# Five of each expert's 84 weight halves as native fp32 matmuls, in a kernel that splits every weight into two fp32r parts

## The chip, the cores and the metric

The kernel runs on one core of one Trainium2 chip. The metric is the device time of one execution in microseconds. Of the kernel before three runs are given, 1871.48, 1871.95 and 1874.96 us, with a median of 1871.95 us.

## The reference, cut to what matters

Two decoder blocks are applied to 256 tokens of 1024 features, in fp32: a hybrid layer (convolution, two kinds of attention, a state-space branch, and a feed-forward), then a retention layer with a dense feed-forward and a Fourier layer with a mixture of experts. The change lies in that last part alone:

```
def moe_swiglu(h, w_router, w_gate, w_up, w_down):
    t = h.reshape(-1, d)
    logits = (t @ w_router).astype(jnp.float32)
    top_val, top_idx = lax.top_k(logits, TOP_K)          # 2 of 8 experts
    top_w = jax.nn.softmax(top_val, axis=-1)
    ...
    for e in range(N_EXPERTS):
        out = out + gates[:, e:e + 1] * swiglu(t, w_gate[e], w_up[e], w_down[e])
```

An expert has a gate and an up matrix of 1024 x 3584 and a down matrix of 3584 x 1024, so 44 MB of fp32 weights; `swiglu(t)` is `(silu(t @ w_gate) * (t @ w_up)) @ w_down`.

## The kernel before

**Weights.** They arrive as units of 128 x 2048 fp32 (1 MB) in a ring of raw tiles, in the order of use: 42 units, 84 halves of 128 x 1024, for an expert. `split` (line 117) turns a half into two fp32r tiles: ScalarE copies it to `wh` (line 128), VectorE subtracts, `wl = raw - wh` (line 129). The tiles come from the pool `wp` with four buffers of each (`WB = 4`, line 77), so the wh of a half can be written once TensorE has read the wh of the split half four before it. After the second half of a unit, `fetch` (line 94) has SP issue the next unit into the raw tile that comes free. `half` (line 171) splits one half more and hands out the oldest of the queue `wq`.

**Order.** The instructions of TensorE and SP stand as the program writes them; a scheduler sets those of VectorE and ScalarE.

**An expert.** `gather` (line 1075) builds one-hot matrices `so` from the routing (four VectorE operations, line 1082) and with them picks the expert's tokens, up to 128, as `ex` (hi and lo part, 8 blocks of features). Its pieces are called by hooks at halves 77 to 83 of the expert before. `experts` (line 1116) then runs seven rounds s = 0 to 6:
- `gate_strip(s)`: halves g0 to g3, each with two of the eight feature blocks. `hi_lo` (line 1133) makes three matmuls of 128 x 512 for a block: ex-hi with wh (line 1142), ex-lo with wh (1143), ex-hi with wl (1144). Between g1 and g2 of round s stands `turn(s - 1)`, the transposes of the round before (lines 1194 and 1196). ScalarE evacuates the sum as `sg` (line 1177).
- `up_strip(s)`: halves u0 to u3; VectorE evacuates it as `h` = up x sg (line 1184).
- `down(s - 1)`: halves d0 to d3, with the turned tokens `hx` (lines 1200 and 1201) of the round before.

So the halves run g, u, then six times g, u, d, and d of round 6 last. Up and down halves exist in two forms on TensorE, chosen at run time by the expert's count of tokens (`either`, line 1146): over 64 tokens, three matmuls a block as in the gate; else the hi and lo part of the tokens lie beside each other in one stationary operand, and two matmuls do (lines 1139 and 1144). Gate halves always have three. Below, the second kind of expert is called packed, and the halves of round s are written g0 to g3, u0 to u3, d0 to d3 (the d halves that run in a round belong to round s - 1). `combine` (line 1246) adds an expert's result to `acc`, as hooks at halves 4 and 8 of the next expert: two matmuls (lines 1251 and 1252) and a VectorE operation (line 1254) for each of two token tiles. Experts are counted from 0.

Native fp32 matmuls, of unsplit tiles, already stand in other places, such as line 786 in the retention layer (128 x 512, both operands fp32).

Of the kernel before, what the change touches and what calls it, by code (L numbers as in the profile page):

```python
# [9 lines left out]
F32 = mybir.dt.float32  # L10
F32R = mybir.dt.float32r
I32 = mybir.dt.int32
AF = mybir.ActivationFunctionType
# [3 lines left out]
P = 128  # L17
# [5 lines left out]
E = 8  # L23
# [3 lines left out]
UE = 42  # L27
# [36 lines left out]
def kernel(  # L64
# [10 lines left out]
    nc = tc.nc  # L75
    NU = ws_d.shape[0]
# [2 lines left out]
    HQ = 512  # L79
    HU = UN // 2  # L80

    NRAW, R2N, R3N, R4N = 6, 4, 2, 2
    const = ctx.enter_context(tc.tile_pool(name="const", bufs=1))
    rawp = ctx.enter_context(tc.tile_pool(name="rawp", bufs=NRAW))
# [5 lines left out]
    raw = []  # L90
    wq = []
# [23 lines left out]
    half_ = [0, 0]  # L115

    def split(scales=None, between=None):


        if not raw or (half_[1] == H_F2 and scales is None):  # L120
            return
        half_[1] += 1
        r = raw[0][0][:, half_[0] * HU:(half_[0] + 1) * HU]
        wh = wp.tile([P, HU], F32R, tag="wh", name="wh")
        wl = wp.tile([P, HU], F32R, tag="wl", name="wl")
        if scales is None:
            for o in (slice(0, HQ), slice(HQ, HU)) if half_[1] == 1 else (slice(0, HU),):
                nc.scalar.activation(out=wh[:, o], in_=r[:, o], func=AF.Copy)  # L128
                nc.vector.tensor_tensor(out=wl[:, o], in0=r[:, o], in1=wh[:, o].bitcast(F32), op=ALU.subtract)  # L129
                if between is not None and o.start == 0:  # L130
                    between()
        else:
            for t in range(2):
                o = slice(t * 512, t * 512 + 512)
                nc.scalar.activation(out=wh[:, o], in_=r[:, o], func=AF.Copy, scale=scales[:, t:t + 1])
                nc.vector.scalar_tensor_tensor(out=wl[:, o], in0=r[:, o], scalar=scales[:, t:t + 1],
                                               in1=wh[:, o].bitcast(F32), op0=ALU.mult, op1=ALU.subtract)
        wq.append((wh, wl))
        if half_[0]:
            fetch(raw.pop(0)[1])  # L140
        half_[0] ^= 1
# [39 lines left out]
    def bank(tag="mm", shape=(P, 2, S)):  # L181
        return psp.tile(list(shape), F32, tag=tag, name=tag, bufs={"mm": 4, "sd": 2, "dn": 2}[tag])

    mm = nc.tensor.matmul
# [175 lines left out]
    start = ExitStack()  # L360
# [12 lines left out]
    with pa:  # L373
# [264 lines left out]
        for i in range(8):  # L638
            ps = unitT(xh, xl)
            c, h = divmod(i, 2)  # L640
# [28 lines left out]
        for c in range(4, KD, 2):  # L669
            gg = []  # L670
            for _ in range(2):
                g = B.tile([P, 4, S], F32, tag="gate2", name="gate2")
                for h in range(2):
                    ps = unitT(xh, xl)
# [63 lines left out]
    with ExitStack() as pr:  # L738
# [120 lines left out]
        for c in range(KD):  # L859
            ps = bank("mm", (P, S))  # L860
# [23 lines left out]
    with ExitStack() as pn:  # L884
# [90 lines left out]
        for cc in range(4):  # L975
            ps = unit_late(zh, zl) if cc == 0 else unitT(zh, zl)
# [34 lines left out]
        for c in range(0, KD, 2):  # L1011
            ps, o = to_tok(xT_, c, "mm")
            nc.scalar.activation(out=acc[:, :, o], in_=ps, func=AF.Copy)

        ps = bank("sd", (P, 3, E))
# [51 lines left out]
    with ExitStack() as pe:  # L1067
# [7 lines left out]
        def gather(posc, posuc):  # L1075

            so = G2.tile([P, 2, P], F32R, tag="so", name="so")
            for t in range(2):  # L1080
                for c, o in ((posc, slice(0, HS)), (posuc, slice(HS, P))):
                    nc.vector.tensor_scalar(out=so[:, t, o], in0=iota1[:, o], scalar1=c(t), scalar2=None, op0=ALU.is_equal)
            ex = G.tile([P, KD, 2, P], F32R, tag="ex", name="ex")
            sot = G2.tile([P, 2, P], F32R, tag="sot", name="sot")
            rs = G2.tile([P, 1], F32, tag="rsl", name="rsl")

            xs = {}

            def rows(hf):
                o = slice(hf * 512, hf * 512 + 512)  # L1090
                ps = bank("sd", (P, 512))
                for i, (src, t) in enumerate(((th, 0), (th, 1), (tl, 0), (tl, 1))):
                    mm(ps, so[:, t], src[:, t, o], start=i == 0, stop=i == 3)
                xs[hf] = G2.tile([P, 512], F32, tag=("sg", "h")[hf], name="xs", bufs=1)
                nc.scalar.activation(out=xs[hf], in_=ps, func=AF.Copy)

            def tokens_of(hf):
                ps = bank("sd", (P, 4, P))
                for b in range(4):
                    nc.tensor.transpose(ps[:, b], xs[hf][:, b * P:(b + 1) * P], ident)  # L1100
                ks = slice(4 * hf, 4 * hf + 4)
                nc.scalar.activation(out=ex[:, ks, 0], in_=ps, func=AF.Copy)
                nc.vector.tensor_tensor(out=ex[:, ks, 1], in0=ps, in1=ex[:, ks, 0].bitcast(F32), op=ALU.subtract)  # L1103

            def rest():
                ps = bank("sd", (P, 2 * P + 2))
                for t in range(2):
                    mm(ps[:, t * P:(t + 1) * P], so[:, t], identr, start=True, stop=True)
                for t in range(2):
                    mm(ps[:, 2 * P:2 * P + 1], so[:, t].bitcast(F32), rcol[:, t:t + 1], start=t == 0, stop=t == 1)  # L1110
                nc.vector.tensor_copy(out=rs, in_=ps[:, 2 * P:2 * P + 1])
                nc.vector.tensor_copy(out=sot.rearrange("p a b -> p (a b)"), in_=ps[:, 0:2 * P])

            return ex, sot, rs, [lambda: rows(0), lambda: tokens_of(0), lambda: rows(1), lambda: tokens_of(1), rest]

        def experts(ex, rs, half_fn, hooks=None, n_of=None):

            pd = [bank("dn", (P, 512)) for _ in range(2)]
            n = [0]
            few = [None]
# [2 lines left out]
            def nexth(**kw):  # L1127
                if hooks and n[0] in hooks:
                    hooks[n[0]]()
                n[0] += 1  # L1130
                return half_fn(**kw)

            def hi_lo(x, items, packed):

                for out_, k, wh, wl, first, last in items:
                    xk = x[:, k].rearrange("p a b -> p (a b)")
                    if packed:
                        e = xk[:, HS:HS + P]
                        mm(out_, e, wh, start=first, stop=False)  # L1139
                    else:  # L1140
                        e = xk[:, 0:P]
                        mm(out_, e, wh, start=first, stop=False)  # L1142
                        mm(out_, xk[:, P:2 * P], wh, start=False, stop=False)  # L1143
                    mm(out_, e, wl, start=False, stop=last)  # L1144
# [10 lines left out]
            def strip_items(ps, h, w):  # L1155
                return [(ps, 2 * h + kk, w[0][:, kk * 512:(kk + 1) * 512], w[1][:, kk * 512:(kk + 1) * 512],
                         h + kk == 0, h == 3 and kk == 1) for kk in range(2)]

            def strip(mid=None):
                ps = bank("mm", (P, 512))  # L1160
                for h in range(4):
                    if h == 2 and mid is not None:
                        mid()
                    hi_lo(ex, strip_items(ps, h, nexth()), False)
                return ps

            def pair(f):
# [100 lines left out]
        for e in range(E):  # L1268
            ex, sot, rs, _ = nxt
# [246 lines left out]
```

## Time and profile before

| what | value |
|---|---|
| median of three runs | 1871.95 us |
| the profiled execution | 1872.74 us, span 1871.0 us |
| granted TensorE clock, mean | 0.995 of full speed |
| TensorE busy | 1817.4 us, 97% of the span |
| VectorE busy | 1482.0 us, 79% |
| ScalarE busy | 1210.6 us, 65% |
| expert stage | from about 900 us to the end |
| moved from memory | 502.45 MB |

In the rows, PE is TensorE, DVE is VectorE, ACT is ScalarE and SP issues the DMAs; PEld is TensorE's loading of stationary operands. Matmuls are pipelined: a matmul row shows about 0.39 us, and the next one starts some 0.23 us after it, so durations of TensorE are taken from start to start. A native fp32 matmul shows as two records.

### The profile page before, as it was taken

The page shows a single profiled execution, that of the slowest core. Times are in us where ns is not written, and L with a number is a line of the kernel's source. Part 1 is how long each engine was busy: PE and PEld are TensorE (multiplying, and loading weights), DVE is VectorE, ACT ScalarE, POOL GpSimd, SP SyncE. Part 2 cuts the span into 40 slices and gives each one's busy share as a digit, 9 for nine tenths or more (in the row PEclk, how much of TensorE's full clock was granted, in tenths as well). Part 3 has the DMA queues.
Part 4 walks back from the last instruction along what each step waited for, and adds up shares of the span by engine and source line. Part 5 has one row for each costly group of instructions (what it writes and reads, how often), then busy time and mean ns, then how long its engine had stood idle before and what let it go on. Part 6 is the DMA issues. An engine that isn't in the chain of part 4 may idle for free. (4 is left out here: it accounts for less than half of the span.)

```text
span 1871.0 us, 28740 instructions
## 1 busy us (share of the span) xinstructions
PE 1817.4 (97%) x10890; PEld 1574.5 (84%) x10890; DVE 1482.0 (79%) x1855; ACT 1210.6 (65%) x1484; POOL 158.2 (8%) x154
## 2 busy tenths in 40 slices
PE   8999999999999999999999999999999999999997
PEld 7999999999888999998777887777777788888885
DVE  5666676657677666656899989999999998988987
ACT  5765454455344444446787777888878777777775
POOL 2302122211111122110000000000000000000000
PEclk9999999999999999999999999999999999999999
DMA  8344544555444564544799998999999999999970
GB/s 313 140 154 168 193 178 183 181 181 197 158 150 159 189 248 184 187 170 180 295 419 377 353 367 326 411 386 377 415 354 413 381 353 364 332 356 354 343 290 36
DMA packets 71156, 505.77 MB, mean 270 GB/s; under 512 B 7888, under 2 KB 8016, under 8 KB 10320
## 3 DMA queue, kind: packets, MB, share of 16 engines
q1 hardware_dynamic: 70992, 503.53, 70.7%
q8 instruction: 110, 1.80, 0.4%
q14 instruction: 54, 0.44, 0.1%
HBM read 502.45 MB, written 1.05 MB: 269 GB/s over the span
## 5 line engine op out<-in xcount | busy, mean ns | idle before, releaser
L129 DVE TENSOR_TENSOR wl<-raw,wh 128x1024 fp32r<-128x1024 f32 (+1 forms) x906 | 1078.5, 1227 | 235.3 <-ACT wh L128 226.2
L128 ACT ACTIVATE wh<-raw 128x1024 fp32r<-128x1024 f32 (+1 forms) x906 | 922.0, 1053 | 428.9 <-PE mm L190 188.7
L189 PE MATMUL mm<-xh,wh 128*128 128x256 f32 x1248 | 357.5, 286 | 6.7 <-ACT xh L342 6.7
L1144 PE MATMUL mm<-wl,ex 128*128 128x512 f32 x896 | 356.0, 397 | 3.7 <-DVE wl L129 3.7
L190 PE MATMUL mm<-xl,wh 128*128 128x256 f32 x1248 | 355.2, 285 | 1.0 <-DVE xl L343 0.7
L191 PE MATMUL mm<-xh,wl 128*128 128x256 f32 x1248 | 354.9, 284 | 0.8 <-DVE wl L129 0.8
L1142 PE MATMUL mm<-wh,ex 128*128 128x512 f32 x672 | 270.4, 402 | 0.0
L1143 PE MATMUL mm<-wh,ex 128*128 128x512 f32 x672 | 266.1, 396 | 0.2 <-DVE ex L1103 0.2
L189 PEld LDWEIGHTS mm<-xh,wh 128*128 128x128 f32 x1248 | 237.9, 191 | 8.2 <-ACT xh L342 6.7
L190 PEld LDWEIGHTS mm<-xl,wh 128*128 128x128 f32 x1248 | 237.9, 191 | 2.4 <-DVE xl L343 2.3
L191 PEld LDWEIGHTS mm<-xh,wl 128*128 128x128 f32 x1248 | 237.7, 190 | 1.1 <-DVE wl L129 1.0
L1144 PEld LDWEIGHTS mm<-wl,ex 128*128 128x128 f32 x896 | 168.6, 188 | 54.2 <-DVE wl L129 13.7
L1144 PE MATMUL dn<-wl,hx 128*128 128x512 f32 x448 | 183.6, 410 | 12.1 <-DVE wl L129 11.9
L1143 PEld LDWEIGHTS mm<-wh,ex 128*128 128x128 f32 x672 | 126.7, 189 | 28.2 <-DVE ex L1103 0.5
L1142 PEld LDWEIGHTS mm<-wh,ex 128*128 128x128 f32 x672 | 126.6, 188 | 26.0 <-ACT wh L128 0.3
L1144 PEld LDWEIGHTS dn<-wl,hx 128*128 128x128 f32 x448 | 84.2, 188 | 55.8 <-DVE wl L129 40.1
L190 PE MATMUL mm<-hl,wh 128*128 128x256 f32 x352 | 99.8, 283 | 0.0
L191 PE MATMUL mm<-hh,wl 128*128 128x256 f32 x352 | 99.8, 283 | 0.0
L189 PE MATMUL mm<-hh,wh 128*128 128x256 f32 x352 | 99.8, 283 | 0.0
L1139 PE MATMUL dn<-wh,hx 128*128 128x512 f32 x224 | 89.2, 398 | 0.0
L1142 PE MATMUL dn<-wh,hx 128*128 128x512 f32 x224 | 88.9, 397 | 0.0
L1139 PE MATMUL mm<-wh,ex 128*128 128x512 f32 x224 | 88.7, 396 | 0.0
(400 smaller groups left out, 2500.7 us busy)
## 6 DMA issues: line engine op xcount, KB each, us to landing
raw<-in_ws_dram SPq DMA_DIRECT2D x451, 1024.0 KB, 6.3
xT<-in_ws_dram SPq DMA_DIRECT2D x22, 1024.0 KB, 7.0
raw<-in_ws_dram SPq DMA_DIRECT2D x3, 512.0 KB, 6.3
xT<-in_xT_dram SPq DMA_DIRECT2D x4, 256.0 KB, 5.4
xT<-in_xT_dram SPq DMA_DIRECT2D x1, 1024.0 KB, 8.3
out_dram<-acc SPq DMA_DIRECT2D x4, 256.0 KB, 2.1
cstA<-in_cst_dram SPq DMA_DIRECT2D x1, 576.0 KB, 9.1
raw<-in_ws_dram SPq DMA_DIRECT2D x2, 256.0 KB, 4.5
```

The costliest lines, as they stand in the source:

```text
L128: nc.scalar.activation(out=wh[:, o], in_=r[:, o], func=AF.Copy)
L129: nc.vector.tensor_tensor(out=wl[:, o], in0=r[:, o], in1=wh[:, o].bitcast(F32), op=ALU.subtract)
L189: mm(ps, wh[:, c], xh, start=start, stop=False)
L190: mm(ps, wh[:, c], xl, start=False, stop=False)
L191: mm(ps, wl[:, c], xh, start=False, stop=stop)
L1139: mm(out_, e, wh, start=first, stop=False)
L1142: mm(out_, e, wh, start=first, stop=False)
L1143: mm(out_, xk[:, P:2 * P], wh, start=False, stop=False)
L1144: mm(out_, e, wl, start=False, stop=last)
```

## The change

In each expert the half g1 of rounds 1 to 5 is not split. `split` puts the raw half itself into the queue, and the gate strip multiplies it with a fp32 copy `ef` of the two feature blocks that this half needs, one native matmul for a block. `ef` is written by ScalarE when the tokens are gathered. To make room for it, `so` has one buffer instead of two.

```
+    WHOLE = [8 + 12 * (s - 1) + 1 for s in range(1, 6)]
+    H_MOE = 2 * (NU - E * UE)
...
         r = raw[0][0][:, half_[0] * HU:(half_[0] + 1) * HU]
+        if (half_[1] - 1 - H_MOE) % (2 * UE) in WHOLE and half_[1] > H_MOE:
+
+            wq.append((r, None))
+            if half_[0]:
+                fetch(raw.pop(0)[1])
+            half_[0] ^= 1
+            return
...
-            so = G2.tile([P, 2, P], F32R, tag="so", name="so")
+            so = G.tile([P, 2, P], F32R, tag="so", name="so")
...
+            ef = G.tile([P, 2, P], F32, tag="ef", name="ef")
...
+                if hf == 0:
+                    nc.scalar.activation(out=ef, in_=ps[:, 2:4], func=AF.Copy)
...
-                    hi_lo(ex, strip_items(ps, h, nexth()), False)
+                    w = nexth()
+                    if w[1] is None:
+                        for kk in range(2):
+                            mm(ps, ef[:, kk], w[0][:, kk * 512:(kk + 1) * 512], start=False, stop=False)
+                    else:
+                        hi_lo(ex, strip_items(ps, h, w), False)
```

On TensorE, the gate strip of round 2 in expert 2, g0 and g1 and the turn behind them. Before (wh_13487 and wl_13488 are g0's tiles, wh_13512 and wl_13513 are g1's):

```order
L1142 MATMUL mm_13518<-wh_13487,ex_11432 128x512
L1143 MATMUL mm_13518<-wh_13487,ex_11432 128x512
L1144 MATMUL mm_13518<-wl_13488,ex_11432 128x512
L1142 MATMUL mm_13518<-wh_13512,ex_11432 128x512
L1143 MATMUL mm_13518<-wh_13512,ex_11432 128x512
L1144 MATMUL mm_13518<-wl_13513,ex_11432 128x512
L1142 MATMUL mm_13518<-wh_13512,ex_11432 128x512
L1143 MATMUL mm_13518<-wh_13512,ex_11432 128x512
L1144 MATMUL mm_13518<-wl_13513,ex_11432 128x512
L1150 COMPARE_AND_BRANCH
L1196 MATMUL sd_13541<-cst_71,h_13455 128x128 x4
```

The first three rows are g0's second block, the next six are g1. In the same place of the changed kernel:

```order
L1158 MATMUL mm_13417<-wh_13390,ex_11396 128x512
L1159 MATMUL mm_13417<-wh_13390,ex_11396 128x512
L1160 MATMUL mm_13417<-wl_13391,ex_11396 128x512
L1183 MATMUL mm_13417<-raw_12967,ef_11397 128x512 x2
L1166 COMPARE_AND_BRANCH
L1217 MATMUL sd_13436<-cst_71,h_13358 128x128 x4
```

Six matmuls of g1 have become two, which read the raw tile and ef.

On VectorE, where round 0 of expert 5 ends and round 1 begins. Before (wl_17071, wl_17096, wl_17113 and wl_17123 belong to g0 to g3 of round 1, wl_17148 to its u0; acc is the second half of the expert before; h is round 0's):

```order
L129 TENSOR_TENSOR wl_17071<-raw_16563,wh_17070 128x1024
L1150 UNCONDITIONAL_BRANCH
L129 TENSOR_TENSOR wl_17096<-raw_16563,wh_17095 128x1024
L1254 SCALAR_TENSOR_TENSOR acc_9283<-sd_17104,gts_9926,acc_9283 128x512
L1254 SCALAR_TENSOR_TENSOR acc_9283<-sd_17108,gts_9926,acc_9283 128x512
L129 TENSOR_TENSOR wl_17113<-raw_16594,wh_17112 128x1024
L1184 SCALAR_TENSOR_TENSOR h_17101<-mm_17030,rsl_15586,sg_17018 128x512
L129 TENSOR_TENSOR wl_17123<-raw_16594,wh_17122 128x1024
L1150 UNCONDITIONAL_BRANCH
L129 TENSOR_TENSOR wl_17148<-raw_16627,wh_17147 128x1024
```

In the changed kernel (wl_16884 is g0, wl_16922 g2, wl_16932 g3, wl_16953 u0):

```order
L140 TENSOR_TENSOR wl_16884<-raw_16374,wh_16883 128x1024
L1166 UNCONDITIONAL_BRANCH
L1275 SCALAR_TENSOR_TENSOR acc_9283<-sd_16913,gts_9926,acc_9283 128x512
L1275 SCALAR_TENSOR_TENSOR acc_9283<-sd_16917,gts_9926,acc_9283 128x512
L140 TENSOR_TENSOR wl_16922<-raw_16405,wh_16921 128x1024
L140 TENSOR_TENSOR wl_16932<-raw_16405,wh_16931 128x1024
L1205 SCALAR_TENSOR_TENSOR h_16910<-mm_16843,rsl_15437,sg_16831 128x512
L140 TENSOR_TENSOR wl_16953<-raw_16438,wh_16952 128x1024
```

g1's subtraction is gone, and h has moved from behind g2's to behind g3's. Experts 1 to 6 have this move. Expert 7 keeps h behind g2's; expert 0 has it behind g3's too, but no acc pair in front.

On VectorE, the start of expert 5 in the changed kernel: the four so operations of the next gather. Before, they stood in round 1, between u3's and d0's subtractions (so_18348, of the gather after next, as so had two buffers):

```order
L129 TENSOR_TENSOR wl_17198<-raw_16658,wh_17197 128x1024
L1082 TENSOR_SCALAR so_18348<-cst_71,pos_9859 128x64
L1082 TENSOR_SCALAR so_18348<-cst_71,posu_9860 128x64
L1082 TENSOR_SCALAR so_18348<-cst_71,pos_9859 128x64
L1082 TENSOR_SCALAR so_18348<-cst_71,posu_9860 128x64
L129 TENSOR_TENSOR wl_17204<-raw_16675,wh_17203 128x1024
```

Now they stand among round 0's gate halves (wl_16743 is g1 of round 0, wl_16788 and wl_16798 are g2 and g3; y is the result of the expert before):

```order
L1093 TENSOR_SCALAR so_16775<-cst_71,pos_9859 128x64
L1093 TENSOR_SCALAR so_16775<-cst_71,posu_9860 128x64
L140 TENSOR_TENSOR wl_16743<-xT_69,wh_16742 128x1024
L1093 TENSOR_SCALAR so_16775<-cst_71,pos_9859 128x64
L1093 TENSOR_SCALAR so_16775<-cst_71,posu_9860 128x64
L1253 TENSOR_TENSOR y_16758<-dn_15438,y_16758 128x512
L1253 TENSOR_TENSOR y_16772<-dn_15439,y_16772 128x512
L140 TENSOR_TENSOR wl_16788<-raw_16286,wh_16787 128x1024
L140 TENSOR_TENSOR wl_16798<-raw_16286,wh_16797 128x1024
```

The four operations have moved ahead of the gate subtractions of round 0, in experts 1 to 6; the y pair now stands ahead of g2's. In the rounds 2 to 5 the order on VectorE and ScalarE is the same but for g1, and hx, which has moved from between u0's and u1's subtractions to behind u1's; sg stands between u3's and d0's copies and h between d2's and d3's subtractions as before.

## Rows read from the trace of the kernel before

**Rows 1.** The page: busy us, share of the span, instructions; and one costliest group.
```profile
PE 1817.4 (97%) x10890; PEld 1574.5 (84%) x10890; DVE 1482.0 (79%) x1855; ACT 1210.6 (65%) x1484; POOL 158.2 (8%) x154
...
L1139 PE MATMUL mm<-wh,ex 128*128 128x512 f32 x224 | 88.7, 396 | 0.0
```

**Rows 2.** Busy time by stretch (rounds of a packed, then an unpacked expert); the first row names the columns.
```profile
core 0: us, PE busy (x) PEld busy (x) DVE busy (x) ACT busy (x) POOL busy (x), PEclk, DMA share, GB/s
1180.58:1241.45 60.87, 58.49 (x258) 44.76 (x258) 60.26 (x57) 50.93 (x57) 0.00 (x0) 1.00 1.01 414
...
1073.73:1125.35 51.62, 51.62 (x230) 41.88 (x229) 46.01 (x44) 39.46 (x42) 0.00 (x0) 1.00 0.99 367
```

**Rows 3.** Timeline of VectorE, expert 1 (unpacked), two h evacuations: start us, us, what.
```profile
1073.73 0.75 DVE L1184 SCALAR_TENSOR_TENSOR h<-mm,rsl,sg 128x512 f32<-128x512 f32 x1
...
1090.93 0.75 DVE L1184 SCALAR_TENSOR_TENSOR h<-mm,rsl,sg 128x512 f32<-128x512 f32 x1
```

**Rows 4.** Timeline of VectorE, one round of expert 2 (packed).
```profile
1195.79 0.75 DVE L1184 SCALAR_TENSOR_TENSOR h<-mm,rsl,sg 128x512 f32<-128x512 f32 x1
...
1207.59 3.50 DVE L129 TENSOR_TENSOR wl<-raw,wh 128x1024 fp32r<-128x1024 f32 x3
1211.00 0.74 DVE L1184 SCALAR_TENSOR_TENSOR h<-mm,rsl,sg 128x512 f32<-128x512 f32 x1
1211.66 2.35 DVE L129 TENSOR_TENSOR wl<-raw,wh 128x1024 fp32r<-128x1024 f32 x2
```

**Rows 5.** Waits in 1180.58 to 1241.45 (expert 2): us in total, times, longest us.
```profile
ACT wh L128 <- PE mm L1143: 9.8, 12, 1.9
```

**Rows 6.** Timeline of TensorE, the same round; in brackets idle time before and its releaser.
```profile
1197.72 0.51 PE L1144 MATMUL dn<-wl,hx 128*128 128x512 f32 x1 [0.60 <-DVE wl L129]
...
1204.54 0.39 PE L1143 MATMUL mm<-wh,ex 128*128 128x512 f32 x1
...
1205.01 0.40 PE L1139 MATMUL mm<-wh,ex 128*128 128x512 f32 x1
...
1212.93 0.50 PE L1144 MATMUL dn<-wl,hx 128*128 128x512 f32 x1 [0.59 <-DVE wl L129]
```

**Rows 7.** Timeline of ScalarE, the same round.
```profile
1204.97 1.06 ACT L128 ACTIVATE wh<-raw 128x1024 fp32r<-128x1024 f32 x1 [0.34 <-PE mm L1143]
1205.94 0.67 ACT L1177 ACTIVATE sg<-mm,rsl 128x512 f32<-128x512 f32 x1
1206.51 2.00 ACT L128 ACTIVATE wh<-raw 128x1024 fp32r<-128x1024 f32 x2
```

**Rows 8.** Waits of SP's queue, 900 us to the end.
```profile
SPq L101 <- DVE wl L129: 771.8, 318, 4.7
```

**Rows 9.** Timeline of TensorE in the retention layer, native fp32 matmuls of line 786.
```profile
473.31 1.88 PE L786 MATMUL sd<-v,sT 128*128 128x512 f32 x4
474.63 0.80 PE L225 MATMUL mm<-wh,xh 128*128 128x512 f32 x1
475.26 0.39 PE L226 MATMUL mm<-wh,xl 128*128 128x512 f32 x1
```

**Rows 10.** Timeline of VectorE, round 1 of expert 2: first of four so, and what follows them.
```profile
1161.28 0.26 DVE L1082 TENSOR_SCALAR so<-cst,pos 128x64 fp32r<-128x64 f32 x1
...
1161.93 1.23 DVE L129 TENSOR_TENSOR wl<-raw,wh 128x1024 fp32r<-128x1024 f32 x1
```

**Rows 11.** Timeline of VectorE, expert 6, end of round 0.
```profile
1619.18 1.41 DVE L1254 SCALAR_TENSOR_TENSOR acc<-sd,gts,acc 128x512 f32<-128x512 f32 x2 [0.15 <-PE sd L1252]
1620.51 1.22 DVE L129 TENSOR_TENSOR wl<-raw,wh 128x1024 fp32r<-128x1024 f32 x1
1621.64 0.74 DVE L1184 SCALAR_TENSOR_TENSOR h<-mm,rsl,sg 128x512 f32<-128x512 f32 x1
```

**Rows 12.** Timeline of TensorE, the same place: last gate matmul before the turn, and the turn.
```profile
1622.01 0.39 PE L1144 MATMUL mm<-wl,ex 128*128 128x512 f32 x1
1622.44 0.66 PE L1196 MATMUL sd<-cst,h 128*128 128x128 f32 x4
```

**Rows 13.** Timeline of TensorE, start of expert 5, the wl of g3 in round 0.
```profile
1485.07 0.50 PE L1144 MATMUL mm<-wl,ex 128*128 128x512 f32 x1 [0.40 <-DVE wl L129]
```

More of the change, by code (lines that the diff above doesn't have):

```diff
@@ L1112, in rest, with experts @@
                 nc.vector.tensor_copy(out=sot.rearrange("p a b -> p (a b)"), in_=ps[:, 0:2 * P])
-            return ex, sot, rs, [lambda: rows(0), lambda: tokens_of(0), lambda: rows(1), lambda: tokens_of(1), rest]
-        def experts(ex, rs, half_fn, hooks=None, n_of=None):
+            return (ex, ef), sot, rs, [lambda: rows(0), lambda: tokens_of(0), lambda: rows(1), lambda: tokens_of(1), rest]
+        def experts(exf, rs, half_fn, hooks=None, n_of=None):
+            ex, ef = exf
             pd = [bank("dn", (P, 512)) for _ in range(2)]
```

## The prediction, made before the changed kernel ran

> **What bounds the kernel now.** I read the page's busy shares first: TensorE 97%, VectorE 79%, ScalarE 65% of the span [rows 1]. The change touches only the expert stage, so the question is what binds there, and the busy time by stretch shows two kinds of expert [rows 2]. The first stretch lies in an expert with few tokens (packed up and down products, line 1139): VectorE is busy 60.26 of 60.87 us, TensorE 58.49. The second lies in an expert with more than 64 tokens: TensorE is busy all of 51.62 us, VectorE 46.01. Line 1139's mm form has 224 rows [rows 1], and a packed expert has 56 (28 up halves of two), so four experts are packed; by where those rows stand in time they are 0, 2, 3, 4, and 1, 5, 6, 7 are unpacked.
>
> In an **unpacked** expert one round (the s-loop's gate strip g0 to g3, up strip u0 to u3, down halves d0 to d3) takes 17.20 us, from one h evacuation to the next [rows 3]. TensorE is the bound and VectorE has slack.
>
> In a **packed** expert a round takes 15.21 us, from h at 1195.79 to h at 1211.00 [rows 4]. VectorE looks like the bound. But it is not free-running: ScalarE waits 9.8 us in four rounds for a TensorE matmul of line 1143, the one that frees a buffer of the four in wp [rows 5]. Follow one round in time:
> - TensorE gets d3's wl at 1197.72 after a stop of 0.60 us, runs without a gap through d3, g0, g1, the turn, g2, and reads g3's wh for the last time in the matmul at 1204.54, which ends at 1204.93 [rows 6].
> - At 1204.97 ScalarE starts the wh of u3 after idling for exactly that matmul (g3, u0, u1, u2 hold all four buffers). The evacuation sg follows at 1205.94, d0's wh at 1206.51 [rows 7].
> - VectorE starts d0's wl at 1207.59, when that wh is there, then d1, d2, h at 1211.00, d3 at 1211.66, done at 1212.88 [rows 4].
> - TensorE gets d3's wl at 1212.93 [rows 6], 15.21 us after the last time.
>
> So the round is a **closed chain**: 7.21 us of TensorE (1197.72 to 1204.93), then 8.00 us of ScalarE and VectorE. VectorE's own work only nearly fills the same time. What lies in TensorE's stretch lengthens the round; VectorE work outside u3 to d3 is not on the chain.
>
> DMA is not a bound: SP's issues wait for VectorE to free a raw buffer (318 times, 771.8 us in all, [rows 8]).
>
> **The change part by part.** *A native half instead of a split one, on TensorE.* A split half is six matmuls. Two of them start 0.47 us apart (1204.54 to 1205.01 [rows 6]), so six take 1.40 us. The native form has a row: line 786 multiplies unsplit fp32 tiles at 128x512. Two such matmuls show as four records from 473.31; the next matmul starts with the last record, and the one after it at 475.26; taking off that one's own 0.23, the four take 1.72 us [rows 9]. So a native half costs TensorE 0.32 us more. Bounds: not below 0.32, since those four records already run back to back at 0.43 us each; up to 0.42, if the half is followed by the extra 0.1 us that a matmul has after a stop (0.51 instead of 0.39 in [rows 6]). I take 0.32, since the row is the same operation at the same size.
>
> The Trainium skill, "TensorE: Matmul & The Clock Gate", section "Back-to-back issue gap", gives 216 ns for a 512-column matmul at full clock; an estimate by that has a split half at 1.30 us, a native one of eight passes at 1.73, and the rounds below at 13.8 us in sum instead of 10.2. The rows have 0.233 us for the split matmuls, so the measured 0.32 stands.
>
> *Rounds 2 to 5, all experts.* In unpacked experts TensorE is the bound: +0.32 a round. In packed ones the native half is g1, inside TensorE's 7.21 us: the round becomes 15.53. The wh and wl that fall away are g1's, outside the 8.00 us; u3 still waits for g3's buffer, because g1 is not among the four halves between. So nothing comes back. 8 experts x 4 rounds x 0.32 = **+10.2 us**.
>
> *Round 1 and the way into it.* Two more moves show in the order. VectorE's h of round 0 stands behind g1.2 before; in the changed kernel, behind g1.2 and g1.3 (experts 1 to 6). And the four so operations of the next gather, 0.65 us together [rows 10], stand in front of g0's last wl instead of round 1's d0. In unpacked experts the second acc pair waits 0.15 us for TensorE's combine, after which wl and h follow without a gap [rows 11], and the turn waits for h: TensorE's last gate matmul starts at 1622.01, the turn at 1622.44, 0.20 later than its stream would have it [rows 12]. VectorE gains nothing by having no g1.1, since acc waits for TensorE; one more wl before h is 1.13 us (a third of the 3.41 from 1207.59 to 1211.00 [rows 4]). That delay contains round 1's 0.32.
> - Expert 7: neither move; the turn's wait hides all but 0.12 of the 0.32. +0.1.
> - Expert 6: +1.13.
> - Experts 1 and 5, behind a packed one: TensorE already stops 0.40 us for g0's last wl [rows 13]; four so in front add 0.65. With the 1.13: +1.78 each, +3.6.
> - Experts 2 to 4: h up to 1.13 late, and up to 0.65 comes back where the so were: between 0.48 and 1.13, I take 0.8 each, +2.4.
> - Expert 0: h is late already by more than 0.32, and no acc stands there: 0.
>
> Together **+7.2 us**; bounds 0 (if h stays where it is in time) and 8 x 1.78 = 14.
>
> *Small ones.* The ef copy (ScalarE, 128x256, 8 times) is at most the 0.67 us of an evacuation of 128x512 [rows 7], and ScalarE is busy 50.93 of 60.87 us: covered by its waits for TensorE; without that cover at most 5 us. The 40 wh copies that go are hidden likewise. A raw unit with a native half is given back by TensorE instead of VectorE, some halves later, and the issues behind it on SP wait too; prefetch covers it, as no wl or wh waits for a DMA there: 0.
>
> **Sum**: the profiled execution took 1872.74 us (span 1871.0); 1872.74 + 10.2 + 7.2 = 1890.1. It lies 0.8 above the median of 1871.95, so against that I forecast **1889 us**.
>
> **Rivals.** *VectorE is the bound of packed experts, and the change relieves it (faster).* For it: 99% busy there [rows 2]. Each of 20 packed native halves would then save between 0.28 us (TensorE's idle (60.87 - 58.49) / 4 = 0.60 less 0.32) and 1.13 us (a whole wl). Half way, 0.7 x 20 = 14 us, less 20 x 0.32 = 6.4 for unpacked experts: -7.6, so 1864 (ends 1873 and 1856). It decides if u3's wh can start before g3's last read. Against it: the closed chain, whose pieces fill the 15.21 us to 0.01. The Trainium skill, "Perfetto Trace Analysis", section "Identifying the Most-Contended Engine", makes VectorE's occupancy a fair measure of how close it is to its limit and would have that engine relieved first; by that rule this rival would win. Chance 0.13.
>
> *It cancels (no change).* If the chain gives about 0.3 us a packed half, unpacked losses of 6.4 are just paid. Between the other two, with no mechanism of its own: 0.05.
>
> *Only the matmuls cost.* If the moved h and so change nothing, 40 x 0.32 = 12.8, less what round 1's turn waits hide: 1882; if the packed chain gives the 0.32 back too, 6.4: 1878. Chance 0.15, slower like the forecast.
>
> *The change does not do what it says*: TensorE's order has 40 native pairs, five in each expert, each in g1 of rounds 1 to 5; I give this nothing.
>
> **How the numbers follow.** Forecast 0.67, only the matmuls 0.15, VectorE 0.13, cancelling 0.05. The likeliest gives 1889. Low end 1876: under the 1878 of the third rival. High end 1894: 0.42 instead of 0.32 in the rounds adds 3.2, and a part of the boundary's upper bound. Left out are the first two rivals, below. A run of this kernel can tell about 0.2% (3.7 us) from no change: faster 0.13, same 0.05, slower 0.82.
>
> **What would show it.** h to h in packed rounds 2 to 5 at 15.5 us, in unpacked ones at 17.5; four records of 0.43 us in each native half; VectorE's busy time down by some 46 us (40 x 1.14) with its idle time up as much in packed experts; ScalarE still waiting for line 1143's successor; a turn in expert 6 that waits about 0.8 us longer for h. I am wrong if packed rounds come out under 15.2, or if the native records are not 0.43 us apart.

## The result and the profile after

| | median us | runs us | profiled execution |
|---|---|---|---|
| before | 1871.72 (four runs) | 1869.99 to 1874.96 | 1872.74, span 1871.0 |
| changed | 1897.64 (four runs) | 1895.39 to 1900.96 | 1895.39, span 1893.6 |

The change makes the kernel slower: ratio 1.0138, 95% interval [1.0116, 1.0159], 25.9 us between the medians. I forecast 1889 (1876 to 1894): the direction is right, the size is 8.6 us short and outside the range.

Busy time on the page of the changed kernel, against [rows 1]:

```profile
PE 1829.7 (97%) x10810; PEld 1555.7 (82%) x10810; DVE 1443.5 (76%) x1815; ACT 1177.4 (62%) x1452; POOL 159.1 (8%) x154
```

VectorE has 38.5 us less to do and TensorE 12.3 more. Stretches with a native half in each round, four rounds of a packed expert (2) and three of an unpacked one (1), against [rows 2]:

```profile
1167.87:1229.99 62.12, 59.73 (x249) 42.74 (x248) 56.41 (x53) 47.73 (x53) 0.00 (x0) 1.00 0.99 395
1057.31:1109.89 52.58, 52.58 (x224) 40.70 (x223) 42.85 (x41) 37.22 (x39) 0.00 (x0) 1.00 0.91 361
```

A packed round became longer, 15.53 us, though VectorE now idles for 5.7 us of the four. In the unpacked ones, three times 17.53, TensorE is busy all the time as before. A packed round on VectorE, h to h, against [rows 4]:

```profile
1183.41 0.74 DVE L1205 SCALAR_TENSOR_TENSOR h<-mm,rsl,sg 128x512 f32<-128x512 f32 x1
...
1198.94 0.74 DVE L1205 SCALAR_TENSOR_TENSOR h<-mm,rsl,sg 128x512 f32<-128x512 f32 x1
```

TensorE in the round after it, against [rows 9]: four records in 1.72 us, 0.43 each, and the turn behind them.

```profile
1203.07 1.88 PE L1183 MATMUL mm<-raw,ef 128*128 128x512 f32 x4
1204.79 1.05 PE L1215 MATMUL sd<-cst,h 128*128 128x128 f32 x8
```

Waits in the four packed rounds, against [rows 5]: ScalarE still waits for TensorE's last read of a wh.

```profile
ACT wh L139 <- PE mm L1159: 11.1, 12, 1.9
...
DVE wl L140 <- ACT wh L139: 5.7, 12, 0.9
```

**Where the 25 us are.** I take the distances between the starts of VectorE's h from both traces (seven in each expert) and add them by place. "Way in" is from the last h of one expert to the second h of the next; the end is from the last h to the end of the span.

| part | before | changed | difference |
|---|---|---|---|
| rounds 2 to 6, experts 0 to 3, 5 to 7 | | | +8.9 |
| rounds 2 to 6, expert 4 | 76.10 | 82.46 | +6.4 |
| ways into experts 1 to 7 | | | +7.9 |
| end | 25.76 | 28.03 | +2.3 |
| expert stage, from expert 0's first h | 956.26 | 981.69 | +25.4 |

The profiled executions differ by 22.65 us, since the expert stage began 2.80 us earlier in that of the changed kernel (first h at 911.91 instead of 914.71). In the profiles of the runs below that start lies between 913.7 and 918.8; in three whose edits touch the expert stage alone (pin4, pin4_h, pin4_h_so) it is 913.74, 917.70 and 916.98. It varies by more than what is looked for, and so I read the stage.

**Expert 4** was not in my sum. Its rounds 3 to 6 take 15.95, 17.11, 17.09 and 16.76 us, where experts 2 and 3 have 15.53 three times and 15.21. There the scheduler gave ScalarE another order from round 3 on (in round 3 itself hx still stands behind u1, and sg already ahead of u3). The copies of halves to wh are written by the names of the halves:

```
experts 0 to 3:              u0 u1 hx u2 u3 sg d0 d1 d2 d3
expert 4, rounds 4 to 6:     u0 hx u1 sg u2 u3 d0 d1 d2 d3
```

ScalarE in round 4 of expert 4:

```profile
1434.97 1.06 ACT L139 ACTIVATE wh<-raw 128x1024 fp32r<-128x1024 f32 x1 [2.07 <-PE mm L1159]
1437.82 0.60 ACT L1221 ACTIVATE hx<-sd 128x512 fp32r<-128x512 f32 x1 [1.78 <-PE sd L1215]
1438.31 1.05 ACT L139 ACTIVATE wh<-raw 128x1024 fp32r<-128x1024 f32 x1
1440.62 0.69 ACT L1198 ACTIVATE sg<-mm,rsl 128x512 f32<-128x512 f32 x1 [1.26 <-PE mm L1160]
1441.20 3.89 ACT L139 ACTIVATE wh<-raw 128x1024 fp32r<-128x1024 f32 x4
```

u1's copy (1438.31) stands behind hx, and hx waits 1.78 us for the turn; u2's (1441.20) stands behind sg, and sg waits 1.26 us for the end of the gate strip. VectorE waits 1.67 us for that copy, and TensorE 0.76 for what VectorE makes of it:

```profile
1442.29 4.63 DVE L140 TENSOR_TENSOR wl<-raw,wh 128x1024 fp32r<-128x1024 f32 x4 [1.67 <-ACT wh L139]
```

```profile
1443.57 0.50 PE L1160 MATMUL mm<-wl,ex 128*128 128x512 f32 x1 [0.76 <-DVE wl L140]
```

The kernel before has this order too, but from round 3 of expert 5 on, in unpacked experts, where TensorE is the bound and it costs nothing: from its first h to the next expert's, expert 5 takes 125.90 us and expert 1, without that order, 126.00.

**The way in**, expert 1 on TensorE: the stop for a wl at the start, 1.31 us where it was 0.40 (as in expert 5, [rows 13]), and the turn, which waits 0.85 us for h:

```profile
1015.62 0.50 PE L1160 MATMUL mm<-wl,ex 128*128 128x512 f32 x1 [1.31 <-DVE wl L140]
```

```profile
1029.62 0.55 PE L1217 MATMUL sd<-cst,h 128*128 128x128 f32 x3 [0.85 <-DVE h L1205]
```

VectorE at the second place, against [rows 11]: two subtractions between the acc pair and h, where there was one.

```profile
1025.23 1.41 DVE L1275 SCALAR_TENSOR_TENSOR acc<-sd,gts,acc 128x512 f32<-128x512 f32 x2 [1.53 <-PE sd L1273]
1026.56 2.35 DVE L140 TENSOR_TENSOR wl<-raw,wh 128x1024 fp32r<-128x1024 f32 x2
1028.82 0.74 DVE L1205 SCALAR_TENSOR_TENSOR h<-mm,rsl,sg 128x512 f32<-128x512 f32 x1
```

**The end**: the last work of VectorE, first before, then changed. Between the two rows VectorE's sequencer branches over the overflow path, which this input does not need; 1.84 us have become 4.10.

```profile
1863.15 0.16 DVE L295 SCALAR_TENSOR_TENSOR fr<-rs,rsy 128x2 f32<-128x2 f32 x1
1865.16 2.74 DVE L1348 SCALAR_TENSOR_TENSOR acc<-acc,fr,xT 128x512 f32<-128x512 f32 x4 [1.84 <-DVEq L1310]
```

```profile
1883.52 0.16 DVE L306 SCALAR_TENSOR_TENSOR fr<-rs,rsy 128x2 f32<-128x2 f32 x1
1887.79 2.74 DVE L1369 SCALAR_TENSOR_TENSOR acc<-acc,fr,xT 128x512 f32<-128x512 f32 x4 [4.10 <-DVEq L1331]
```

### The profile page after: what moved, and what is told of

It is laid out like the page before. It is cut to its first block, busy times and chain, and to the rows that moved or that the text cites. A ratio compares the mean times of both kernels' runs of the same rounds, so it can differ in the third digit from the quotient of the medians.

```text
span 1893.6 us, 28447 instructions
## 1 busy us (share of the span) xinstructions
PE 1829.7 (97%) x10810; PEld 1555.7 (82%) x10810; DVE 1443.5 (76%) x1815; ACT 1177.4 (62%) x1452; POOL 159.1 (8%) x154
## 5 line engine op out<-in xcount | busy, mean ns | idle before, releaser
L140 DVE TENSOR_TENSOR wl<-raw,wh 128x1024 fp32r<-128x1024 f32 (+1 forms) x866 | 1034.4, 1225 | 276.8 <-ACT wh L139 266.9
L139 ACT ACTIVATE wh<-raw 128x1024 fp32r<-128x1024 f32 (+1 forms) x866 | 881.7, 1052 | 428.0 <-PE mm L201 186.1
L1160 PE MATMUL mm<-wl,ex 128*128 128x512 f32 x816 | 325.3, 399 | 9.9 <-DVE wl L140 9.8
L1158 PE MATMUL mm<-wh,ex 128*128 128x512 f32 x592 | 238.5, 403 | 0.0
L1159 PE MATMUL mm<-wh,ex 128*128 128x512 f32 x592 | 234.1, 395 | 0.1
L1160 PEld LDWEIGHTS mm<-wl,ex 128*128 128x128 f32 x816 | 153.2, 188 | 60.2 <-DVE wl L140 23.3
L1159 PEld LDWEIGHTS mm<-wh,ex 128*128 128x128 f32 x592 | 111.4, 188 | 24.7 <-DVE ex L1116 0.4
L1158 PEld LDWEIGHTS mm<-wh,ex 128*128 128x128 f32 x592 | 111.5, 188 | 22.6 <-ACT wh L139 0.3
L1155 PE MATMUL mm<-wh,ex 128*128 128x512 f32 x224 | 88.8, 396 | 0.0
```

## The experiments

All runs in one table. The ratio is to the kernel before on the same chip; rounds are h to h in the profile (rounds 2 to 5); "stage" is from expert 0's first h to the end; "jump" is the time from VectorE's branch over the overflow path to the next record of its sequencer.

| run | median us | ratio, 95% interval | packed | unpacked | stage | jump |
|---|---|---|---|---|---|---|
| before | 1871.7 to 1873.5 | | 15.21 | 17.20 | 956.26 | 0.59 |
| changed | 1897.64 | 1.0138 [1.0116, 1.0159] | 15.53, 17.1 in expert 4 | 17.52 | 981.69 | 2.85 |
| no_native | 1878.50 | 1.0028 [1.0018, 1.0037] | 15.22 | 17.21 | 961.17 | 0.60 |
| pin4 | 1893.87 | 1.0111 [1.0094, 1.0128] | 15.53 | 17.52 | 976.87 | 2.87 |
| pin4_h | 1888.28 | 1.0074 [1.0058, 1.0091] | 15.53 | 17.53 | 970.32 | 3.01 |
| pin4_h_so | 1884.60 | 1.0051 [1.0034, 1.0068] | 15.53 | 17.53 | 966.29 | 3.03 |
| g3_native | 1878.76 | 1.0027 [1.0015, 1.0038] | 14.94 | 17.53 | 961.44 | 2.90 |
| wb5_before | 1869.55 | 0.9973 [0.9963, 0.9983] | 14.88 | 17.20 | 950.16 | 3.01 |
| wb5_after | 1939.85 | 1.0352 [1.0334, 1.0370] | 14.83, round 5 up to 28.2 | 17.53 | 1019.68 | 3.15 |
| wb5_after_b | 1874.62 | 1.0009 [0.9999, 1.0019] | 14.83 | 17.53 | 955.28 | 2.98 |
| reordered_before | 1874.39 | 1.0003 [0.9994, 1.0011] | 15.19 | 17.20 | 956.35 | 2.85 |
| shifted_code | 1898.58 | 1.0131 [1.0115, 1.0146] | as changed | 17.53 | 979.57 | 0.59 |
| wb5_reordered | 1870.22 | 0.9984 [0.9975, 0.9993] | 14.88 | 17.20 | 949.97 | 3.03 |
| wb5_late_tile | 1870.04 | 0.9988 [0.9979, 0.9997] | 14.88 | 17.20 | 949.70 | 2.85 |

**No half unsplit (no_native).**

```
-    WHOLE = [8 + 12 * (s - 1) + 1 for s in range(1, 6)]
+    WHOLE = []
```

> The changed kernel with no half unsplit: so keeps its single buffer and the ef copy is still made, though nobody reads it. The order has h behind g1.2's subtraction again; the four so stay ahead of the gate subtractions of round 0. Theory (the native halves and the orders they bring cost nearly all): rounds back at 15.21 us in packed experts and 17.20 in unpacked ones; what is left is so, some 0.65 us in experts 1, 5 and 6, so about 2 us over the kernel before: 1874 us. Rival (the shared so buffer and the ef copy are the larger part): 1885 us or more, with rounds 15.21 and 17.20 but the ways into experts still 1 to 2 us longer.

1878.5 us: nearer to the theory than to the rival, and the rounds are back, but 1874 was too low. Rounds are 15.22 and 17.21; expert 4 is like the others. The ways in cost 0.9 us more than before in experts 1, 5 and 6 and 0.33 in 2 to 4, 3.7 in all; another 1.1 us come at the end, behind VectorE's last four acc operations, the first of which starts 19.95 us after the last h, as before; their cause is open. So the moved so operations cost more than their own 0.65 us in experts 1, 5 and 6: the y pair had moved with them, and together they stand ahead of g2's subtraction. TensorE in expert 1 has the same stop as in the changed kernel:

```profile
1017.36 0.50 PE L1160 MATMUL mm<-wl,ex 128*128 128x512 f32 x1 [1.31 <-DVE wl L140]
```

**ScalarE's order in expert 4 pinned (pin4).** The calls that return sg, hx, h, wh and wl are kept in a dictionary `ins`; `behind` adds an edge of order without a wait; `ih` gives a half's number.

```
+    def behind(later, earlier):
+        tc.add_manual_dep(later.ins, earlier.ins.name,
+                          mybir.DependencyInfo(mybir.DependencyClass.NoSync, mybir.DependencyReason.DATA), reason="order")
...
+        for s in range(1, 7):
+            behind(ins["hx", 4, s - 1], ins["wh", ih(4, s, "u", 1)])
+            behind(ins["sg", 4, s], ins["wh", ih(4, s, "u", 3)])
```

> The changed kernel with ScalarE's order in expert 4 pinned to what experts 2 and 3 have (hx behind u1's copy, sg behind u3's copy). Theory (expert 4's long rounds come from sg standing ahead of the copies of u2 and u3): its rounds 3 to 6 go from 15.95, 17.11, 17.09, 16.76 us to 15.53, 15.53, 15.53, 15.21, so 5.1 us less than the changed kernel. Rival (those rounds are long for another reason, such as transfers that come late there): the rounds stay above 16.5 and the time stays.

Expert 4's rounds are 15.53, 15.53, 15.54, 15.53, 15.22; from its first to its last h it takes 88.02 us instead of 93.12, 5.10 less. Expert 4 now takes as long as experts 2 and 3, so the order was the whole of its extra cost; sg and hx were pinned together, and which of the two costs what was not tried. ScalarE at the same place has u2, u3, sg in this order again, with short waits:

```profile
1440.55 1.06 ACT L144 ACTIVATE wh<-raw 128x1024 fp32r<-128x1024 f32 x1 [0.57 <-PE mm L1164]
1441.95 1.06 ACT L144 ACTIVATE wh<-raw 128x1024 fp32r<-128x1024 f32 x1 [0.34 <-PE mm L1164]
1442.91 0.67 ACT L1203 ACTIVATE sg<-mm,rsl 128x512 f32<-128x512 f32 x1
```

**h ahead of g3's subtraction (pin4_h).**

```
+        for e in range(1, 7):
+            behind(ins["wl", ih(e, 1, "g", 3)], ins["h", e, 0])
```

> As the run before it, and in experts 1 to 6 VectorE's h of round 0 pinned ahead of g1.3's subtraction, where it stood before the change. Theory (TensorE's turn waits for h, which the change put one subtraction later): the turn's stop falls from about 0.85 us to under 0.1 in experts 1, 5 and 6, so 1 us each; 0.35 us each in experts 2 to 4; about 4 us in all below the run with expert 4 pinned. Rival (VectorE does the same work before the turn, and g3 then comes as much later): within 1 us of that run.

The stage is 6.55 us shorter than with expert 4 pinned alone, 5.6 in the medians: more than expected, because experts 2 to 4 gain as much as the others, 1.1 us each (in experts 5 and 6 some 0.4 of it in the way in and 0.7 in round 2). In expert 1 the turn follows the native half without a stop:

```profile
1032.68 1.88 PE L1188 MATMUL mm<-raw,ef 128*128 128x512 f32 x4
1034.39 0.60 PE L1222 MATMUL sd<-cst,h 128*128 128x128 f32 x4
```

**so back in its place (pin4_h_so).** The four operations of the next gather are called where they were, kept in `ins` by the number of the gather (`ng`), and pinned between u3's and d0's subtractions of round 1.

```
-                    nc.vector.tensor_scalar(out=so[:, t, o], in0=iota1[:, o], scalar1=c(t), scalar2=None, op0=ALU.is_equal)
+                    ins["so", ng[0], t, o.start] = nc.vector.tensor_scalar(out=so[:, t, o], in0=iota1[:, o], scalar1=c(t), scalar2=None, op0=ALU.is_equal)
...
+        for e in range(1, E - 1):
+            for t in range(2):
+                for o in (0, HS):
+                    behind(ins["so", e + 1, t, o], ins["wl", ih(e, 1, "u", 3)])
+                    behind(ins["wl", ih(e, 1, "d", 0)], ins["so", e + 1, t, o])
```

> As the run before it, and the four so operations put back where they stood before the change, between u3's and d0's subtractions of round 1 (still one buffer). Theory: TensorE's stop for g0's wl at the start of experts 1, 5 and 6 falls back from 1.3 or 1.0 us to about 0.4, some 0.7 to 0.9 us each, and 0.4 each in experts 2 to 4, so 3 to 4 us below the run before it; what is then left over the kernel before is the native matmuls in the rounds alone, 10 us, rounds at 15.53 and 17.52. Rival (the ways into experts are long because of the ef copy or the single buffer): no change against the run before it.

The stop at the start of expert 1 is 0.40 us again, the stage 4.0 us shorter, 3.7 in the medians, as expected. The 10.0 us that are left in the stage are not the rounds alone, as I had said: they are 9.8 in the rounds 2 to 6 and 2.4 at the end, less 2.2 by which the ways in are now shorter than before the change.

**The native half at another place (g3_native).**

```
-    WHOLE = [8 + 12 * (s - 1) + 1 for s in range(1, 6)]
+    WHOLE = [8 + 12 * (s - 1) + 3 for s in range(1, 6)]
...
-                if hf == 0:
+                if hf == 1:
                     nc.scalar.activation(out=ef, in_=ps[:, 2:4], func=AF.Copy)
...
-                            mm(ps, ef[:, kk], w[0][:, kk * 512:(kk + 1) * 512], start=False, stop=False)
+                            mm(ps, ef[:, kk], w[0][:, kk * 512:(kk + 1) * 512], start=False, stop=kk == 1)
```

> The native half is g3 of rounds 1 to 5 instead of g1 (ef holds those two blocks), with ScalarE's and VectorE's order in packed experts pinned to that of experts 2 and 3. Theory (closed chain in packed rounds: u3's copy waits for the last read of the split half four before it): with g3 unsplit that half is g2, read 1.4 us earlier, so the chain no longer decides and TensorE does, with 15.21 - 0.60 + 0.32 = 14.95 us a round, against 15.53 with g1; unpacked rounds stay at 17.52. 16 rounds times 0.58 make some 9 us less than with g1 (run pin4). Rival (VectorE's total work or the matmuls alone set the packed round, wherever the half lies): 15.53 as with g1, and no difference to run pin4 in the rounds.

14.93 to 14.96 us a packed round, where 14.95 was expected. The same edit two halves later makes a packed round 0.27 us shorter than before the change instead of 0.32 longer, so the rival falls. The stage is 15.4 us shorter than with expert 4 pinned alone, where 9 were expected: 9.6 in rounds 2 to 6, and 5.6 in the ways in, since h of round 0 stands behind one gate subtraction again. Waits in four packed rounds: half of the waits for a freed wh are gone (6 for 12), and sg, which waits for the end of the gate strip, is what ends late next.

```profile
ACT wh L144 <- PE mm L1164: 7.9, 6, 1.9
...
ACT sg L1203 <- PE mm L1188: 3.1, 4, 0.9
```

The unpacked experts still lose 0.32 us a round, and the ways in and the end are not mended here, so the whole is 0.27% slower than before.

**Five buffers, without and with the native half (wb5_before, wb5_after, wb5_after_b).**

```
-    WB = 4
+    WB = 5
...
-    NRAW, R2N, R3N, R4N = 6, 4, 2, 2
+    NRAW, R2N, R3N, R4N = 5, 4, 2, 2
```

> The kernel before with five buffers of wh and wl instead of four, paid for with one raw tile (five in the first pool), and the order in packed experts pinned to what it was. The start of the kernel may get longer by the missing raw tile, so only the rounds are read. Theory (closed chain through the fourth buffer): u3's copy then waits for g2's read, so packed rounds fall to VectorE's own work, 60.26 / 4 = 15.06 us, from 15.21; unpacked ones stay at 17.20. Rival (no chain, VectorE is simply the bound at 15.21): 15.21.

14.88 us, below the 15.06 that I had from the busy time of [rows 2]. With the chain open VectorE is busy without a gap:

```profile
1167.27:1226.79 59.52, 57.14 (x257) 44.83 (x256) 59.52 (x57) 50.40 (x57) 0.00 (x0) 1.00 1.01 409
```

59.52 us is what VectorE needs for the same 57 operations, not 60.26: an operation that starts after a stop does not overlap with the one before it (three subtractions in a row take 3.50 us, one alone 1.23 [rows 4, 10]). This kernel beats both, by 0.27% against the one before ([0.9963, 0.9983]).

> The changed kernel (g1 native) with five buffers of wh and wl, one raw tile fewer, order in packed experts pinned. Theory: without the chain through the fourth buffer the native half gives VectorE its 1.13 us back, and TensorE is the bound: packed rounds at 14.95 us instead of 15.53, under the 15.21 of the kernel before; unpacked rounds 17.52. Rival (the native half costs its 0.32 us in a packed round whatever frees the buffers): 15.4 to 15.5.

14.83 us in rounds 2 to 4 of the packed experts, 0.12 below what I expected. Round 5 takes 25.8 to 28.2 us there and about 23 in experts 1, 5 and 6. The native half lies in xT, the one place of the ring that is a fixed tile: split has the next transfer into it issued before the matmuls stand in the program, so they wait for that transfer and take its weights. In this run half g1 of round 5 is thus multiplied by other weights; with the ring of the changed kernel no native half falls there. The four records take 3.62 us instead of 1.88; TensorE had stood still for 10.56 us, and the granted clock from 1242.90 to 1246.60 is 0.55, near the lower of its two levels (1.2 of 2.4 GHz).

```profile
1242.94 3.62 PE L1188 MATMUL mm<-xT,ef 128*128 128x512 f32 x4 [10.56 <-DMA xT<-in_ws_dram]
```

In the next run xT stands elsewhere in the ring.

```
+    xT_flat = xT.rearrange("p a b -> p (a b)")
+    fetch(xT_flat)
     if R4N:
         more_room("raw4p", R4N)
-    xT_flat = xT.rearrange("p a b -> p (a b)")
-    fetch(xT_flat)
```

> The changed kernel with five buffers again, one raw tile fewer, and the tile xT put two places earlier into the ring of raw tiles, so that no native half lies in it (in the earlier run the half of round 5 did; its matmuls then waited for the next transfer into xT, 10.6 us, and took those weights, so that run is read in rounds 1 to 4 only). Theory: all five rounds like rounds 1 to 4 of that run, 14.83 us in packed and 17.53 in unpacked experts, against 14.88 and 17.20 in the kernel before with five buffers: the native half gives nothing to speak of in packed experts and costs its 0.32 us in unpacked ones. Rival (fewer raw tiles make the native halves wait for transfers): round 5 stays long.

The native rounds 2 to 5 of packed experts are at 14.82 to 14.84 us: the same native half that costs 0.32 us a packed round with four buffers gives 0.05 with five. In unpacked experts it costs 0.32 either way, and the whole is 5 us slower than five buffers alone. Four packed rounds:

```profile
1164.49:1223.78 59.29, 57.94 (x249) 43.64 (x248) 56.10 (x53) 47.21 (x53) 0.00 (x0) 1.00 1.00 410
```

VectorE is relieved of 3.4 us here against wb5_before and idles for 3.2, and the rounds gain 0.2 in all; TensorE is busy for 57.94 of 59.29 us. What holds the rounds at 14.83 was not followed further.

**Another order in the kernel before (reordered_before).**

```
+        for e in range(1, E):
+            for t in range(2):
+                behind(ins["acc", e, 1, t], ins["h", e, 0])
+            behind(ins["wl", ih(e, 1, "g", 2)], ins["acc", e, 1, 1])
...
+            for s in range(1, 6):
+                behind(ins["h", e, s], ins["wl", ih(e, s, "d", 3)])
```

> The kernel before, no native half, only the order on VectorE pinned: at the start of an expert h first, then the acc pair, then g2's subtraction (instead of acc pair, g2's, h); in rounds 1 to 5 h behind d3's subtraction instead of ahead of it; ScalarE in expert 4 as in experts 2 and 3. Theory: TensorE's turn in round 1 no longer waits for h (0.8 us each in experts 2 to 4, 0.1 in the others), and in packed rounds the chain loses h's 0.7 us, so that VectorE's own work sets them: 15.06 instead of 15.21, 20 rounds. Together 3 + 3 = 6 us less than the kernel before: 1866 us. Rival (h behind d3 makes the next turn late, and the packed rounds are VectorE-bound already): 15.21 or more and 1870 us or more.

Pinned besides: ScalarE's order in expert 4 as in pin4, so between u3's and d0's subtractions of round 1, and hx's subtraction of round 1 behind u1's. A miss. Packed rounds are 15.19 us, and the median does not move. With h behind d3 TensorE no longer stops for d3's wl but for that of g0, one half later:

```profile
1200.24 0.50 PE L1152 MATMUL mm<-wl,ex 128*128 128x512 f32 x1 [0.37 <-DVE wl L134]
```

h stays on the chain; only the half that closes it is another. Full cycles of experts 2 and 3 (first h to the next expert's first h) are 0.15 and 0.17 us shorter, so the turn's gain at the start was mostly taken back as well.

**VectorE's code moved (shifted_code).**

```
     nc.vector.memset(ones, 1.0)
+    for i in range(75):
+        nc.vector.memset(ones[:, i:i + 1], 1.0)
```

> The changed kernel with 75 one-column memsets of a constant tile on VectorE ahead of its first real work (a time in which VectorE waits for the first transfer), nothing else. Theory (the jump over the unused overflow path near the end takes 2.85 us instead of 0.59 because VectorE's program is some 70 instructions shorter and the jump lies elsewhere in the pages of code that are fetched): put back near its old place, the jump takes 0.6 us again, and the kernel ends 2.3 us earlier. Rival (the jump is longer for another reason, such as the work just before it): 2.85 us as before.

The jump takes 0.59 us again, and the time from the last h to the end is 25.79 us instead of 28.03. The end of this run, to be held against the two above:

```profile
1888.73 0.16 DVE L308 SCALAR_TENSOR_TENSOR fr<-rs,rsy 128x2 f32<-128x2 f32 x1
1890.74 2.74 DVE L1371 SCALAR_TENSOR_TENSOR acc<-acc,fr,xT 128x512 f32<-128x512 f32 x4 [1.84 <-DVEq L1333]
```

The median, 1898.6 of three runs, does not show the 2.3 us; the stage of the profiled run began 5 us later than in the changed kernel's, and three runs cannot tell that from the edit.

**Five buffers with the order at the start (wb5_reordered, wb5_late_tile).** The first has `NRAW, R2N, R3N, R4N = 5, 4, 2, 2`, the second `6, 3, 2, 2`; both pin h, the acc pair, so and hx's subtraction as above, and leave the packed rounds in the order before, with h ahead of d3.

> The kernel before, no native half, five buffers of wh and wl, one raw tile fewer in the first pool, and at the start of an expert h first, then the acc pair, then g2's subtraction. Theory: packed rounds at 14.88 us as with five buffers alone, and another 0.2 to 0.8 us per expert from a turn that does not wait for h: 2 to 3 us below the 1869.6 of the run with five buffers, 1867. Rival (what the turn gains, the next stop takes back, as the reordering alone showed): 1869 to 1870.

> As the run before it, but the raw tile that pays for the fifth buffer is taken from the second pool, which is opened later, instead of the first. Theory (a missing raw tile lengthens the start of the kernel by 1 to 3 us): the expert stage begins that much earlier, 1865. Rival (the start is bound by the memory and not by the ring): no difference to the run before it.

1870.2 and 1870.0 us: the rivals came nearer both times. The stages, 949.97 and 949.70 us, stand beside 950.16 with five buffers alone, and the starts at 917.6 and 916.5 us are within what other runs have. Neither is better than the plain fifth buffer.

## Why the prediction was right or wrong

**The price of a native half: right.** 0.32 us, from four records 0.43 us apart. The rounds with it, without expert 4's disturbed ones, give 10.1 us where the sum had 10.2. The 13.8 by the figure of the Trainium skill ("TensorE: Matmul & The Clock Gate", "Back-to-back issue gap") is not borne out.

**The closed chain: right.** Packed rounds came out at 15.53, unpacked at 17.52, and three runs show that the place of the half and the number of buffers decide, not VectorE's load: 14.94 with the half at g3, 14.88 and 14.83 with five buffers. The first rival (VectorE relieved, faster) falls with them. The Trainium skill's "Perfetto Trace Analysis", "Identifying the Most-Contended Engine", would relieve the busiest engine; here VectorE was busy 99% of a packed round, lost 1.1 us of work, and the round grew. With the chain opened by a fifth buffer VectorE is busy 59.52 of 59.52 us, as a bound is; but there too taking the 1.1 us off it gave 0.05 us a round.

**"8 experts x 4 rounds x 0.32": the step that failed.** It rests on the statement ahead of the prediction that the order in rounds 2 to 5 is the same but for g1 and hx. I had read that in expert 2. In expert 4 it is false: sg and hx moved ahead of copies on ScalarE from round 3 on. Its rounds 3 to 6 took 15.95, 17.11, 17.09 and 16.76 us in place of 15.53 three times and 15.21. That costs 5.1 us, all of it given back by pinning the order.

**The ways in, +7.2: nearly right in sum (7.9), less so in its parts.** Experts 2 to 4 were forecast at 0.8 each and measured 0.79, 0.80, 0.78, which is luck in part: I had the so operations as a gain there of up to 0.65, and moved they cost 0.33 (run no_native). Experts 7 and 0 were forecast at 0.1 and 0 (0.06 and -0.01). Experts 1 and 5, 1.78 each, measured 2.00 and 1.46. Expert 6 was forecast at 1.13 and measured 2.04: I left out the so operations there, though the order had them, and they cost 0.92 (run no_native). The mechanism stands, and the third rival (only the matmuls cost) falls: h one subtraction later costs 1.1 us in each of six experts, so and y some 3.7 in all, and some 2.4 of these 10.3 are given back in round 1; that this comes from g1's missing subtraction I only argue, since it was not tried alone.

**The end, not in the sum: +2.3 us.** It is the second step that failed: no term of my sum covered what lies behind the last h. No row of the trace before told that the jump could be longer; its place in VectorE's program decides it (run shifted_code).

10.1 + 5.1 + 7.9 + 2.3 = 25.4 us of the expert stage, against 17.4 forecast and 25.9 between the medians. With the first of the two missed terms the forecast would have been 1894.1, with both 1896.4. The range ended at 1894 because its upper part held only the bounds of terms that I had listed, and nothing for an order that I had not read everywhere.

Of the smaller signs: VectorE's busy time fell by 38.5 us and not by 46; in the expert stage it now stops 190 times where it stopped 85 times, and an operation behind a stop does not overlap with the one before it. The turn of expert 6 waits for h as said, 0.86 us.

## What to carry to other kernels

Where a scheduler sets an engine's order, a small edit can shift it far from the edit, so compare the order in every repetition of a loop and not in one. A busy share of 99% does not make an engine the bound: follow the buffers to the wait that closes the loop, and put slower work where it is not on that loop (the same edit costs 0.32 us a packed round at g1 and gains 0.27 at g3). Compare stages between marks in the trace where the start of a kernel varies by more than the effect.

## What the runs showed of the hardware

VectorE's branch over the overflow path took 0.59 or 0.60 us in three kernels and 2.85 to 3.15 in eleven. In the changed kernel its place in VectorE's program decides that: 75 small instructions far ahead of it brought 2.85 back to 0.59, with the same code around it. In the other kernels this was not tried. The Trainium skill, "Runtime: NRT & Kernel Launch", "Instruction fetch mechanics", says that a taken branch to code outside the window already loaded has to wait for that code; the shifted run agrees, with 2.26 us for it, though no row shows the code being loaded. How far the code must be shifted was not tried.
